# Conditioning vectors 2 to 8 in jobs of 512 columns with raw buffers of their own

## The chip, the cores and the metric

The kernel runs on one core of one Trainium2 chip. A core has TensorE (PE, matrix products into PSUM), VectorE (DVE), ScalarE (ACT), GpSimd (POOL) and SyncE (SP), which here issues nearly all DMAs from one queue, in order. PEld is PE's weight load, which overlaps its matmuls. The metric is the device time of one execution in microseconds (us), lower is better.

## The reference

One layer of a diffusion backbone over 512 latent tokens and 256 context tokens, all float32, with model width 1024 and feed-forward width 2816. Nine conditioning vectors of width 1024 (shift, scale and gate for each of three sub-layers) come from one matrix:

```python
def adaln(cond, w_mod, b_mod):
    m = jax.nn.silu(cond) @ w_mod + b_mod
    return jnp.split(m, N_MOD, axis=-1)

def ffn_sublayer(h, mods, pre_g, post_g, w_gate, w_up, w_down):
    shift, scale, gate = mods
    y = swiglu(modulate(rms_norm(h, pre_g), shift, scale), w_gate, w_up, w_down)
    return h + 0.5 * gate * rms_norm(y, post_g)
```

The layer is a first feed-forward on latent and context tokens (vectors 0 to 2), a mixer of attention and convolution (3 to 5), and a second feed-forward on latent tokens alone (6 to 8). The latent tokens are conditioned by `c`, the context tokens by `c_ctx`. Vectors 0 and 1 are needed at once. Vectors 2, 3 and 4 are needed for both conditions, 5 to 8 for the latent one only.

## The kernel before

**Precision.** Each float32 product is made of three matmuls on float32r halves: `hi` (line 62, ScalarE) rounds a tensor, `lo` (line 67, VectorE) takes the rest, and `wx` (line 92) multiplies hi by hi, hi by lo and lo by hi. Every weight tile therefore goes through a DMA into a raw buffer (tag `wraw`, 4 buffers of 128x1024), a ScalarE copy (`whi`, 4 buffers), a VectorE subtraction (`wlo`, 4 buffers), and then PE. `unit` (line 74) does this; its DMA is line 77.

**Order.** The tile framework builds each engine's list of instructions itself. It goes by the order in which the code is written and by its own estimates of when operands and buffers are free, so an instruction can run ahead of its place. On the chip each engine and SyncE's queue then work through their list in order.

**The first feed-forward.** The 22 chunks of 128 hidden columns form groups of 6, 6, 6 and 4. `gate_up1(f)` (line 405) makes chunk f: weights `f1gu`, sums `pa`, `pb` (latent, 512 columns) and `pc` (context, 256 columns), then silu, product, and the halves `hh` and `hl`. After a group, the first chunk of the next group is made, and then the down-projection adds the group's part of the eight output blocks: the loop over `d` at line 517, with weights `f1d` and sums in PSUM tags `pd` and `pc`, two buffers each, emptied by VectorE into `yl` and `yc` (lines 523 to 527). In the last group, chunks 20 and 21 are made for the context columns first (shorter matmuls), then the context blocks are projected (line 531), chunks 20 and 21 are made for the latent columns (line 540), and the latent blocks follow (line 554). Meanwhile the context's norm, residual and modulation run as `chain` (`sandwich`, line 1026).

**The conditioning of vectors 2 to 8.** It isn't a matmul: for one column block, VectorE multiplies each of the eight raw row blocks of the matrix by a column of `sc` (silu of the condition, one number per partition) and adds them up; PE then sums over the partitions by multiplying with ones; and VectorE picks each column's sum by a product with the identity and a reduction. The work is cut into 20 jobs of two accumulators of 256 columns (line 435). For vectors 2 to 4 the two are the latent and the context condition of the same columns (two raw loads of 512 KB). For 5 to 8 they are two column blocks of the latent condition (four raw loads). `mod_unit` (line 439) loads into the `wraw` buffers (line 448), does 16 operations of 256 columns (lines 455 and 458), and splits the result (`mah`, `mal`). `mod_spread` (line 473) does the two matmuls with ones into a `pd` buffer, two masked products (line 480) and two sums (line 484), and, at a vector's last block, adds the bias and makes the scale or gate. `mod_step` (line 467) spreads the job before and begins the next one. It is called after each of the chunks 2 to 21, twice after chunk 4 (line 512).

Of the kernel before, what the change touches and what calls it, by code (L numbers as in the profile page):

```python
# [16 lines left out]
P = 128  # L17
DM = 1024
ND = 8
# [20 lines left out]
class Builder:  # L40
# [142 lines left out]
    def build(self):  # L183
# [248 lines left out]
            self.lo(hl[:, c0:c1], a[:, c0:c1], hh[:, c0:c1])  # L432
            return h

        mod_jobs = [[(m, d, 0), (m, d, 1)] for m in (2, 3, 4) for d in range(0, ND, 2)]
        mod_jobs += [[(m, d, 0), (m, d + 2, 0)] for m in (5, 6, 7, 8) for d in (0, 4)]
        pend = []

        def mod_unit():

            job = mod_jobs.pop(0)
            acc = self.t(fp, [P, 2, 256], "macc")
            raws = {}
            for hf in range(2):
                for i, (m, d, v) in enumerate(job):
                    if (m, d, hf) not in raws:
                        raw = raws[m, d, hf] = self.t(self.wp, [P, DM], "wraw", bufs=self.n_raw)
                        nc.sync.dma_start(out=raw, in_=io["wmod"][8 + (m - 2) * 4 + d // 2, hf])
                    raw = raws[m, d, hf]
                    for k in range(4):  # L450
                        kk = hf * 4 + k
                        s = sc[:, 2 * kk + v:2 * kk + v + 1]
                        src = raw[:, k * 256:k * 256 + 256]
                        if kk == 0:
                            nc.vector.tensor_scalar(out=acc[:, i], in0=src, scalar1=s,
                                                    scalar2=None, op0=ALU.mult)
                        else:
                            nc.vector.scalar_tensor_tensor(out=acc[:, i], in0=src, scalar=s,  # L458
                                                           in1=acc[:, i], op0=ALU.mult,
                                                           op1=ALU.add)  # L460
            ah = self.t(fp, [P, 2, 256], "mah", F32R)
            al = self.t(fp, [P, 2, 256], "mal", F32R)
            self.hi(ah, acc)
            self.lo(al, acc, ah)
            pend.append((job, ah, al))

        def mod_step():
            if pend:
                mod_spread(*pend.pop(0))
            if mod_jobs:  # L470
                mod_unit()

        def mod_spread(job, ah, al):
            pm = self.t(psf, [P, 2, 256], "pd", bufs=2)
            self.mm(pm, self.ones_r, ah, True, False)
            self.mm(pm, self.ones_r, al, False, True)
            for i, (m, d, v) in enumerate(job):
                mods = (ml, mcx)[v]
                j = self.t(fp, [P, 2, P], "mdj")
                nc.vector.tensor_tensor(  # L480
                    out=j, in0=pm[:, i].rearrange("p (i n) -> p i n", i=2),
                    in1=self.ident.unsqueeze(1).to_broadcast([P, 2, P]), op=ALU.mult)
                c0 = m * 8 + d
                nc.vector.tensor_reduce(out=mods[:, c0:c0 + 2], in_=j, axis=AX.X, op=ALU.add)
                if d != 6:
                    continue
                nc.vector.tensor_tensor(
                    out=mods[:, m * 8:m * 8 + 8], in0=mods[:, m * 8:m * 8 + 8],
                    in1=vec[:, V_BM + m * 8:V_BM + m * 8 + 8], op=ALU.add)
                if m == 2:  # L490
                    make_gate((gp1, gp1c)[v], mods, 2, V_POST1, 0.5)
                elif m == 4:
                    make_scale((sml, smc)[v], mods, 4, V_MPRE)
                elif m == 5:
                    make_gate(gpm, ml, 5, V_MPOST, 1.0)
                elif m == 7:
                    make_scale(s2l, ml, 7, V_PRE2)
                elif m == 8:
                    make_gate(gp2, ml, 8, V_POST2, 0.5)
# [8 lines left out]
        for gi, g in enumerate(groups):  # L508
            for f in g:
                if f not in hs:  # L510
                    hs[f] = gate_up1(f, (f not in late, True))
                for _ in range(0 if f < 2 else 2 if f == 4 else 1):
                    mod_step()
            if gi + 1 < len(groups):
                f = groups[gi + 1][0]
                hs[f] = gate_up1(f)
                for d in range(ND):
# [7 lines left out]
                    else:  # L525
                        nc.vector.tensor_tensor(out=yl[d], in0=yl[d], in1=pl, op=ALU.add)
                        nc.vector.tensor_tensor(out=yc[d], in0=yc[d], in1=pc[:, :NCX], op=ALU.add)
        while mod_jobs or pend:
            mod_step()
        sqyc = self.sqsum(fp, NCX)  # L530
        for d in range(ND):
            w = self.unit(wsl(d), len(g) * P)
# [25 lines left out]
        for half in range(2):  # L558
            c = slice(half * 256, half * 256 + 256)
            for d in range(NFULL, ND):  # L560
                if half == 0:
                    tags = (("hh", HB), ("hl", HB)) if d + 1 < ND else (("macc", 1), ("mah", 1))
                    wd[d] = self.unit(wsl(d), len(g) * P, [
                        self.t(fp, [P, NT], tag, F32R, bufs=bufs) for tag, bufs in tags])
                down1(d, wd[d], c)
# [533 lines left out]
def _layout(inp):  # L1099
# [15 lines left out]
    arr["vec"] = np.ascontiguousarray(np.concatenate(vec, axis=1))  # L1115
    wm = f("w_mod")[0]
    first = wm[:, :2048].reshape(DM, 2, ND, P).transpose(0, 2, 1, 3).reshape(DM, 2048)
    arr["wmod"] = np.concatenate([_wide(first, 8), _wide(wm[:, 2048:], 28)], axis=0)
    for l, n in (("f1", "ffn1"), ("f2", "ffn2")):
        g = _blocks(f(f"{n}_w_gate")[0], NF)  # L1120
        u = _blocks(f(f"{n}_w_up")[0], NF)
# [44 lines left out]
```

## Time and profile before

| | |
|---|---|
| time, 3 runs | 1680.52 us median, 1679.67 to 1681.71 |
| the profiled execution | 1680.81 us, of which the span is 1679.0 |
| mean granted clock of PE | 0.992 |
| conditioning loads from `wmod` into `wraw` | 56 of 512 KB, 3.7 us each from issue to landing |
| conditioning multiply-adds, line 458 | from 64.3 to 553.5 us |
| first feed-forward, chunks and down-projections | about 60 to 620 us |

The lines of the profile that the argument needs stand in the prediction. Three forms occur. A line of a timeline gives start, duration, engine, line, operation, output and inputs, shape and, in brackets, the idle time before it with what ended that. A line of waits gives who waited for whom, total us, how often, and the longest. A line of a group gives the count, the busy us together, the mean ns of one, and the idle time before.

### The profile page before, as it was taken

The page shows a single profiled execution, that of the slowest core. Times are in us where ns is not written, and L with a number is a line of the kernel's source. Part 1 is how long each engine was busy: PE and PEld are TensorE (multiplying, and loading weights), DVE is VectorE, ACT ScalarE, POOL GpSimd, SP SyncE. Part 2 cuts the span into 40 slices and gives each one's busy share as a digit, 9 for nine tenths or more (in the row PEclk, how much of TensorE's full clock was granted, in tenths as well). Part 3 has the DMA queues.
Part 4 walks back from the last instruction along what each step waited for, and adds up shares of the span by engine and source line. Part 5 has one row for each costly group of instructions (what it writes and reads, how often), then busy time and mean ns, then how long its engine had stood idle before and what let it go on. Part 6 is the DMA issues. An engine that isn't in the chain of part 4 may idle for free. (4 is left out here: it accounts for less than half of the span.)

```text
span 1679.0 us, 23556 instructions
## 1 busy us (share of the span) xinstructions
PE 1616.9 (96%) x9154; PEld 1405.3 (84%) x9154; DVE 998.1 (59%) x1699; ACT 647.7 (39%) x1050; POOL 132.3 (8%) x126
## 2 busy tenths in 40 slices
PE   5999999999999988999999999999999999999996
PEld 4887888888888878889888888788889998888886
DVE  5656467456745789577777776473347843343345
ACT  5322122112211556355555555442237732222234
POOL 2100000000000135100000000000002100000003
PEclk9999999999999999999999999999999999999999
DMA  9233333235433547854545442732246743232321
GB/s 374 81 112 101 106 120 105 83 97 193 157 120 103 169 137 243 251 167 124 146 121 163 120 132 95 252 128 96 92 151 195 258 132 120 82 107 91 97 76 51
DMA packets 95248, 232.85 MB, mean 139 GB/s; under 512 B 10912, under 2 KB 34592, under 8 KB 95136
## 3 DMA queue, kind: packets, MB, share of 16 engines
q1 hardware_dynamic: 95136, 231.34, 43.3%
q8 instruction: 72, 1.18, 0.3%
q14 instruction: 40, 0.33, 0.1%
HBM read 201.94 MB, written 16.78 MB: 130 GB/s over the span
## 5 line engine op out<-in xcount | busy, mean ns | idle before, releaser
L62 ACT CAST whi<-wraw 128x1024 fp32r<-128x1024 f32 (+2 forms) x274 | 271.8, 993 | 594.1 <-PE pc L90 174.9
L67 DVE TENSOR_TENSOR wlo<-wraw,whi 128x1024 fp32r<-128x1024 f32 (+2 forms) x264 | 325.8, 1236 | 181.9 <-ACT whi L62 178.1
L90 PE MATMUL pa<-xhi,wlo 128*128 128x512 f32 (+1 forms) x520 | 193.8, 373 | 4.8 <-DVE wlo L67 4.8
L90 PE MATMUL pa<-xhi,whi 128*128 128x512 f32 (+1 forms) x520 | 193.9, 373 | 0.5 <-ACT ob L777 0.5
L90 PE MATMUL pa<-xlo,whi 128*128 128x512 f32 (+1 forms) x520 | 193.3, 372 | 0.0
L90 PE MATMUL pb<-xhi,wlo 128*128 128x512 f32 (+1 forms) x392 | 143.7, 367 | 0.3 <-DVE wlo L67 0.3
L90 PE MATMUL pb<-xhi,whi 128*128 128x512 f32 (+1 forms) x392 | 143.8, 367 | 0.0
L90 PE MATMUL pb<-xlo,whi 128*128 128x512 f32 (+1 forms) x392 | 143.0, 365 | 0.0
L90 PE MATMUL f<-xhi,whi 128*128 128x512 f32 x320 | 127.2, 397 | 0.0
L90 PE MATMUL f<-xhi,wlo 128*128 128x512 f32 x320 | 124.9, 390 | 0.0
L90 PE MATMUL pd<-hh,whi 128*128 128x512 f32 x304 | 121.2, 399 | 3.5 <-ACT hh L62 3.2
L90 PE MATMUL f<-xlo,whi 128*128 128x512 f32 x320 | 124.6, 389 | 0.0
L458 DVE SCALAR_TENSOR_TENSOR macc<-wraw,sc,macc 128x256 f32<-128x256 f32 x280 | 118.4, 481 | 5.3 <-DMA wraw<-wmod 4.3
L90 PE MATMUL pd<-hh,wlo 128*128 128x512 f32 x304 | 120.2, 395 | 0.0
L90 PE MATMUL pd<-hl,whi 128*128 128x512 f32 x304 | 119.2, 392 | 0.0
L90 PE MATMUL pc<-xchi,whi 128*128 128x256 f32 x384 | 109.4, 285 | 4.9 <-ACT whi L62 3.6
L90 PEld LDWEIGHTS pa<-xhi,whi 128*128 128x128 f32 x520 | 98.1, 189 | 17.6 <-ACT ob L777 0.7
L90 PEld LDWEIGHTS pa<-xhi,wlo 128*128 128x128 f32 x520 | 98.4, 189 | 16.7 <-DVE wlo L67 5.5
L90 PE MATMUL pc<-xchi,wlo 128*128 128x256 f32 x384 | 109.3, 285 | 3.0 <-DVE wlo L67 3.0
L90 PE MATMUL pc<-xclo,whi 128*128 128x256 f32 x384 | 109.0, 284 | 0.0
L90 PEld LDWEIGHTS pa<-xlo,whi 128*128 128x128 f32 x520 | 98.2, 189 | 11.6
L90 PEld LDWEIGHTS pc<-xchi,whi 128*128 128x128 f32 x384 | 73.4, 191 | 19.0 <-ACT whi L62 4.0
(313 smaller groups left out, 3287.1 us busy)
## 6 DMA issues: line engine op xcount, KB each, us to landing
wraw<-wmod SPq DMA_DIRECT2D x56, 512.0 KB, 3.7
wraw<-f2gu SPq DMA_DIRECT2D x56, 512.0 KB, 3.5
wraw<-f1gu SPq DMA_DIRECT2D x48, 512.0 KB, 3.8
wraw<-f1d SPq DMA_DIRECT2D x24, 384.0 KB, 3.2
wraw<-f2d SPq DMA_DIRECT2D x24, 384.0 KB, 3.1
wm<-wmod SPq DMA_DIRECT2D x16, 512.0 KB, 9.7
wraw<-wk SPq DMA_DIRECT2D x16, 512.0 KB, 3.9
wraw<-wv SPq DMA_DIRECT2D x16, 512.0 KB, 3.9
```

Source lines behind the costliest of these rows:

```text
L62: self.nc.scalar.copy(out=out, in_=src)
L67: (eng or self.nc.vector).tensor_tensor(out=out, in0=src, in1=hi.bitcast(F32), op=ALU.subtract)
L90: self.nc.tensor.matmul(out, lhsT=lhsT, rhs=rhs, start=start, stop=stop)
L458: nc.vector.scalar_tensor_tensor(out=acc[:, i], in0=src, scalar=s, in1=acc[:, i], op0=ALU.mult, op1=ALU.add)
```

## The change

The jobs get 512 columns. For vectors 2 to 4, a job is half of the row blocks of 512 columns under both conditions (two raw loads, eight operations), so that two jobs make one column block; for 5 to 8, a job is all row blocks of 512 columns under the latent condition (four raw loads, eight operations). There are 12 + 8 = 20 jobs, as before. The raw loads go into a tag of their own, `mraw`, with two buffers, and the accumulators into `vch`, also two. The halves use `tmp` and `sqacc512_0` and `sqacc512_1`, which later work uses too. The spread handles 512 columns with one masked product and one sum of 512; `mod_step` now spreads all that is pending, which is two accumulators after the second job of a pair. Steps are called after chunks 2 to 17, once each, and within the first three down-projections after blocks d=2 and d=5: 22 calls. In the host's layout the matrix for vectors 2 to 8 is a tensor of its own, `wmodr`, in pieces of two row blocks of 512 columns.

```diff
-        mod_jobs = [[(m, d, 0), (m, d, 1)] for m in (2, 3, 4) for d in range(0, ND, 2)]
-        mod_jobs += [[(m, d, 0), (m, d + 2, 0)] for m in (5, 6, 7, 8) for d in (0, 4)]
-        pend = []
+        mod_jobs = [(m, q, (0, 1), r) for m in (2, 3, 4) for q in range(2) for r in ((0, 1), (2, 3))]
+        mod_jobs += [(m, q, (0,), (0, 1, 2, 3)) for m in (5, 6, 7, 8) for q in range(2)]
+        accs, pend = {}, []
...
+            m, q, vs, rs = mod_jobs.pop(0)
+            for v in vs:
+                if rs[0] == 0:
+                    accs[v] = self.t(fp, [P, 512], "vch", bufs=2)
+            for r in rs:
+                raw = self.t(fp, [P, 2, 512], "mraw", bufs=2)
+                nc.sync.dma_start(out=raw, in_=io["wmodr"][(m - 2) * 2 + q, r])
+                for k in range(2):
+                    kk = 2 * r + k
+                    for v in vs:
                         s = sc[:, 2 * kk + v:2 * kk + v + 1]
...
+            if rs[-1] == 3:
+                for v in vs:
+                    ah = self.t(fp, [P, 512], "tmp", F32R, bufs=3)
+                    al = self.t(fp, [P, NT], f"sqacc{NT}_{v}", F32R)
+                    self.hi(ah, accs[v])
+                    self.lo(al, accs[v], ah)
+                    pend.append((m, q, v, ah, al))
 
         def mod_step():
-            if pend:
+            while pend:
                 mod_spread(*pend.pop(0))
...
-        def mod_spread(job, ah, al):
-            pm = self.t(psf, [P, 2, 256], "pd", bufs=2)
+        def mod_spread(m, q, v, ah, al):
+            pm = self.t(psf, [P, 512], "pd", bufs=2)
             self.mm(pm, self.ones_r, ah, True, False)
             self.mm(pm, self.ones_r, al, False, True)
...
+            j = self.t(fp, [P, 512], "tmp", bufs=3).rearrange("p (i n) -> p i n", i=4)
+            nc.vector.tensor_tensor(
+                out=j, in0=pm.rearrange("p (i n) -> p i n", i=4),
+                in1=self.ident.unsqueeze(1).to_broadcast([P, 4, P]), op=ALU.mult)
+            c0 = m * 8 + 4 * q
+            nc.vector.tensor_reduce(out=mods[:, c0:c0 + 4], in_=j, axis=AX.X, op=ALU.add)
+            if q == 1:
...
-                for _ in range(0 if f < 2 else 2 if f == 4 else 1):
+                if 1 < f < NF - 4:
                     mod_step()
...
                         nc.vector.tensor_tensor(out=yl[d], in0=yl[d], in1=pl, op=ALU.add)
                         nc.vector.tensor_tensor(out=yc[d], in0=yc[d], in1=pc[:, :NCX], op=ALU.add)
-        while mod_jobs or pend:
-            mod_step()
+                    if d in (2, 5):
+                        mod_step()
+        assert not mod_jobs and not pend
...
-                    tags = (("hh", HB), ("hl", HB)) if d + 1 < ND else (("macc", 1), ("mah", 1))
+                    tags = (("hh", HB), ("hl", HB)) if d + 1 < ND else (("mraw", 2), ("mraw", 2))
...
-    arr["wmod"] = np.concatenate([_wide(first, 8), _wide(wm[:, 2048:], 28)], axis=0)
+    arr["wmod"] = _wide(first, 8)
+    a = wm[:, 2048:].reshape(4, 2, P, 14, 512).transpose(3, 0, 2, 1, 4)
+    arr["wmodr"] = np.ascontiguousarray(a)
```

More of the change, by code (lines that the diff above doesn't have):

```diff
@@ L433, in gate_up1 @@
             return h
-        mod_jobs = [[(m, d, 0), (m, d, 1)] for m in (2, 3, 4) for d in range(0, ND, 2)]
-        mod_jobs += [[(m, d, 0), (m, d + 2, 0)] for m in (5, 6, 7, 8) for d in (0, 4)]
-        pend = []
+        mod_jobs = [(m, q, (0, 1), r) for m in (2, 3, 4) for q in range(2) for r in ((0, 1), (2, 3))]
+        mod_jobs += [(m, q, (0,), (0, 1, 2, 3)) for m in (5, 6, 7, 8) for q in range(2)]
+        accs, pend = {}, []
         def mod_unit():
[L441 to L451, printed above, removed]
+            m, q, vs, rs = mod_jobs.pop(0)
[8 more added lines that the diff above has]
+                    for v in vs:
@@ L452, in mod_unit @@
                         s = sc[:, 2 * kk + v:2 * kk + v + 1]
-                        src = raw[:, k * 256:k * 256 + 256]
+                        acc = accs[v]
                         if kk == 0:
-                            nc.vector.tensor_scalar(out=acc[:, i], in0=src, scalar1=s,
+                            nc.vector.tensor_scalar(out=acc, in0=raw[:, k], scalar1=s,
                                                     scalar2=None, op0=ALU.mult)
                         else:
-                            nc.vector.scalar_tensor_tensor(out=acc[:, i], in0=src, scalar=s,
-                                                           in1=acc[:, i], op0=ALU.mult,
-                                                           op1=ALU.add)
@@ L461, in mod_unit @@
[L461 to L465, printed above, removed]
+                            nc.vector.scalar_tensor_tensor(out=acc, in0=raw[:, k], scalar=s,
+                                                           in1=acc, op0=ALU.mult, op1=ALU.add)
+            if rs[-1] == 3:
[5 more added lines that the diff above has]
+                    pend.append((m, q, v, ah, al))
@@ L471, in mod_step @@
                 mod_unit()
-        def mod_spread(job, ah, al):
-            pm = self.t(psf, [P, 2, 256], "pd", bufs=2)
+        def mod_spread(m, q, v, ah, al):
+            pm = self.t(psf, [P, 512], "pd", bufs=2)
             self.mm(pm, self.ones_r, ah, True, False)
             self.mm(pm, self.ones_r, al, False, True)
[L477 to L486, printed above, removed]
+            mods = (ml, mcx)[v]
+            j = self.t(fp, [P, 512], "tmp", bufs=3).rearrange("p (i n) -> p i n", i=4)
[5 more added lines that the diff above has]
+            if q == 1:
                 nc.vector.tensor_tensor(
```

## The prediction

> **What bounds the kernel now.** I read the page first, then TensorE's (PE's) busy time by stage, its waits inside the first feed-forward, and the timeline around each wait.
>
> ```profile
> span 1679.0 us, 23556 instructions
> PE 1616.9 (96%) x9154; PEld 1405.3 (84%) x9154; DVE 998.1 (59%) x1699; ACT 647.7 (39%) x1050; POOL 132.3 (8%) x126
> ```
> ```profile
> 0.00:60.00 60.00, 40.67 (x310) 32.11 (x311) 29.99 (x66) 27.69 (x43) 15.90 (x22) 1.00 0.73 282
> 60.00:540.00 480.00, 476.88 (x2707) 415.43 (x2706) 279.67 (x568) 107.74 (x154) 2.16 (x2) 1.00 0.37 118
> 540.00:740.00 200.00, 180.76 (x1146) 163.04 (x1145) 157.56 (x286) 100.61 (x185) 55.97 (x44) 0.97 0.63 192
> ```
>
> The second fence is the view by stretches: after each stretch and its length stand the busy us of PE, PEld, DVE, ACT and POOL, then the granted clock, the DMA share and GB/s. From 60 to 540 us, where nearly all the conditioning work lies, PE idles 480 - 476.88 = 3.1 us. VectorE (DVE) idles 200 us there. So PE bounds this stage, and VectorE time saved is worth nothing unless PE waits for it. From 540 to 740 PE idles 19.2 us, part of it while the last jobs run. The waits from 40 to 580 us are few:
>
> ```profile
> PE pc L90 <- ACT whi L62: 3.6, 1, 3.6
> PE pa L90 <- DVE wlo L67: 2.9, 1, 2.9
> PE pc L90 <- DVE wlo L67: 0.9, 1, 0.9
> ```
>
> The 2.9 us wait is at 143 us, before chunk 6. PE, then ScalarE, then VectorE:
>
> ```profile
> 142.64 0.50 PE L90 MATMUL pd<-hh,whi 128*128 128x512 f32 x1 [0.22 <-ACT whi L62]
> ...
> 143.33 0.28 PE L90 MATMUL pc<-hl,whi 128*128 128x256 f32 x1
> 146.50 0.50 PE L90 MATMUL pa<-xhi,wlo 128*128 128x512 f32 x1 [2.90 <-DVE wlo L67]
> 146.84 0.28 PE L90 MATMUL pc<-xchi,wlo 128*128 128x256 f32 x1
> 147.55 0.28 PE L90 MATMUL pc<-xclo,whi 128*128 128x256 f32 x1
> 147.67 0.40 PE L90 MATMUL pa<-xhi,wlo 128*128 128x512 f32 x1
> ```
> ```profile
> 134.83 1.05 ACT L62 CAST whi<-wraw 128x1024 fp32r<-128x1024 f32 x1
> ```
> ```profile
> 137.70 2.86 DVE L458 SCALAR_TENSOR_TENSOR macc<-wraw,sc,macc 128x256 f32<-128x256 f32 x7
> 145.23 1.22 DVE L67 TENSOR_TENSOR wlo<-wraw,whi 128x1024 fp32r<-128x1024 f32 x1
> ```
>
> The gate weights of chunk 6 had their high part by 135.9 us, but VectorE made the low part only at 145.23, behind the multiply-adds of a third job: chunk 4 has two steps, so three jobs fall on two chunks. PE starts 256-column matmuls 0.12 us apart (147.55 to 147.67), so after 143.33 it was due at 143.45 and went on at 146.50: 3.05 us. The first matmul took 0.34 us to the next one instead of about 0.23, and at 142.64 there is a wait of 0.22 us. In all **3.4 us**.
>
> The 3.6 us wait is at 545 us, before chunk 20, which has only the 256 context columns:
>
> ```profile
> 528.92 6.08 SPq L448 DMA_DIRECT2D wraw<-wmod  x4
> 544.16 2.57 SPq L77 DMA_DIRECT2D wraw<-f1gu  x2
> ```
> ```profile
> 544.77 0.40 PE L90 MATMUL pd<-mal,ones_r 128*128 128x512 f32 x1
> 548.77 0.58 PE L90 MATMUL pc<-xchi,whi 128*128 128x256 f32 x1 [3.60 <-ACT whi L62]
> 550.47 0.58 PE L90 MATMUL pc<-xchi,wlo 128*128 128x256 f32 x1 [0.90 <-DVE wlo L67]
> 554.48 0.31 PE L90 MATMUL pc<-xchi,wlo 128*128 128x256 f32 x1
> ```
> ```profile
> 550.00:555.00 5.00, 4.53 (x23) 4.53 (x24) 4.33 (x8) 2.90 (x4) 0.00 (x0) 0.55 0.56 156
> ```
>
> Four conditioning loads took all four raw slots, so the weights could only be asked for at 544.16, once the multiply-adds had freed a slot. PE was due at 545.00 and started at 548.77 (3.77 us). It then needed 1.70 us for three short matmuls, worth about 0.36 (1.34 more), and from 550.47 to 554.48 it started 18 matmuls 0.22 us apart instead of 0.12 (18 x 0.12 = 2.16, so 1.85 more): after this wait the granted clock was 0.55. Together **7.0 us**.
>
> The queue's own waits say the same for the whole stage: weight loads (L77) wait mostly for conditioning arithmetic.
>
> ```profile
> SPq L77 <- DVE macc L458: 167.4, 35, 20.7
> SPq L448 <- DVE wlo L67: 108.0, 31, 6.3
> ```
>
> **The change part by part.** The profiled execution took 1680.81 us (span 1679.0 and 1.8 around it), 0.3 above the median of 1680.52. The sum is made against 1680.8.
>
> *Arithmetic on VectorE.*
>
> ```profile
> L458 DVE SCALAR_TENSOR_TENSOR macc<-wraw,sc,macc 128x256 f32<-128x256 f32 x280 | 118.4, 481 | 5.3 <-DMA wraw<-wmod 4.3
> L455 DVE TENSOR_SCALAR macc<-wraw,sc 128x256 f32<-128x256 f32 x40 | 13.7, 361 | 13.5 <-DMA wraw<-wmod 13.5
> L171 DVE SCALAR_TENSOR_TENSOR tmp<-x,s,pbs 128x512 f32<-128x512 f32 x4 | 2.8, 750 | 0.0
> L480 DVE TENSOR_TENSOR mdj<-pd,ident 128x256 f32<-128x256 f32 x40 | 16.7, 419 | 1.9 <-PE pd L90 1.9
> ```
>
> Gone are 320 operations of 256 columns, 118.4 + 13.7 = 132.1 us. In their place come 140 multiply-adds and 20 first products of 512. Four such multiply-adds kept VectorE busy 2.8 us (0.70 each), so 140 x 0.70 = 98; the 20 products lie between 0.34 and 0.72 us each, say 0.55, so 11. That saves about 23 us. The 40 masked products become 20, at the 0.69 us of other 512-column operations: 3 us less, and as much for the 40 sums. Some 29 us of VectorE time go, worth **0** directly: the stage's 200 us of idle VectorE time hide it. Without that cover it would be worth 29.
>
> *Matmuls and DMA bytes.* 20 spreads of two 512-column matmuls before (40), 20 after: **0**. The loads stay 56 of 512 KB: **0** as traffic, at a DMA share of 0.37.
>
> *Raw buffers of their own.* The four weight slots no longer wait for conditioning arithmetic. At 545 us there is in addition no job left: the 22 new steps are four for chunks 2 to 5, two in the down-projection, six for chunks 6 to 11, two, six for 12 to 17, two; the twenty jobs end with chunk 17. The 7.0 us wait goes: next late there is weight loading, 512 KB per 24 x 0.12 = 2.9 us of gate or up matmuls, which wraw's four free slots prefetch during the 17 us of chunk 19 (48 rounds of 0.35). Gain between 5 (some of the 0.9 us for the low part and of its slow clock stays) and 7.0; I take **7.0**.
>
> *Steps moved.* Chunk 4 loses its second step, so one job of 16 multiply-adds (16 x 118.4/280 = 6.8 us) fewer stands ahead of the low part at 145.23; it would come at about 138, before 143.45. Gain between 0 and 3.4; I take **3.4**, since 6.8 exceeds 3.05 twice over.
>
> *What the moved steps add.* Steps behind blocks d=2 and d=5 of the down-projections spread into the PSUM tag pd, which has two buffers and also carries those blocks' sums. Nothing of this is in the trace; the nearest rows are one block's end:
>
> ```profile
> 508.00 0.40 PE L90 MATMUL pd<-hh,wlo 128*128 128x512 f32 x1
> 508.23 0.28 PE L90 MATMUL pc<-hh,wlo 128*128 128x256 f32 x1
> 508.35 0.40 PE L90 MATMUL pd<-hh,whi 128*128 128x512 f32 x1
> ```
> ```profile
> 508.43 0.69 DVE L526 TENSOR_TENSOR yl<-yl,pd 128x512 f32<-128x512 f32 x1 [4.16 <-PE pd L90]
> 509.04 0.41 DVE L527 TENSOR_TENSOR yc<-yc,pc 128x256 f32<-128x256 f32 x1
> ```
>
> Today the next block takes the other buffer and has the whole length of a block as slack (18 rounds of 0.23 + 0.12 us, 6.3 us). With one spread between, that block needs the buffer that is emptied until 509.12; PE would be there at 508.35 + 2 x 0.24 = 508.83 and waits 0.3 us. With two spreads the second waits those 0.3, and the block waits for the first one's masked product, behind both additions: 509.4 + 0.7 = 510.1 against 509.6, 0.5 more. By the order of jobs, two spreads fall into the first and the second down-projection each (after chunks 5 and 11, whose jobs end a pair), one more into the second and one into the third: 2 x 0.8 + 2 x 0.3 = 2.2. If VectorE is in the middle of something, up to 0.7 more each; I take **3**, between 0 (the scheduler finds other matmuls to put between) and 4 x 2.9 = 12 (every event as long as the stall at 143).
>
> Sum: 1680.8 - 7.0 - 3.4 + 3 = 1673.4, or **1673** as a median.
>
> [...]
>
> ```profile
> 620.00:660.00 40.00, 35.15 (x281) 33.74 (x281) 37.59 (x79) 21.21 (x50) 20.41 (x19) 1.00 0.71 219
> ```
>
> PE idled 4.85 us of these 40 in many short waits, at a clock of 1.00.
>
> **The rivals.**
>
> *A, the forecast:* both waits go, the PSUM handover costs some 3: 1670 to 1677. 55%.
>
> *B, it does little:* the separate buffers don't separate the loads, since all still go through the one SyncE queue in order, so a conditioning load that waits for one of only two slots holds the weight loads behind it; or the handover costs near its 12. Then only the 7.0 or less remains: 1680.8 - 7.0 + 3 to 12 = 1677 to 1684 (taken to 1684). For it: the 167.4 us of queue waits above exist already. Against: they hardly ever reached PE. 20%.
>
> *C, more than forecast:* the handover costs nothing (1670.4), and the waits behind 580 us shrink too, with VectorE free earlier:
>
> ```profile
> PE pd L90 <- ACT hh L62: 3.2, 1, 3.2
> ```
>
> At 595 us PE waits for the last chunk's hidden values, with VectorE late by the context chain. If that goes, 1667. Against: the context chain's own work, which holds VectorE there, is untouched. 13%.
>
> *D, slower:* jobs of vectors 5 to 8 put four loads through two buffers. The third load waits in SyncE's queue until VectorE has used the first, and the next weights are asked for behind the fourth. Before, the weights of a chunk lay ready 7 to 8 us ahead of PE in these stretches (low part at 375.97, chunk needed at 383.98). If the queue holds them back by more than that, each of the eight jobs costs one stall as at 143, 8 x 3.4 = 27: 1673 + 27 = 1700; with half of them, 1687. Against: four loads stand ahead of the next weights in the same queue today (528.92, then 544.16), and PE waits for it once in the stage, where a chunk is short. 10%.
>
> ```profile
> 375.97 1.23 DVE L67 TENSOR_TENSOR wlo<-wraw,whi 128x1024 fp32r<-128x1024 f32 x1
> 383.98 0.69 DVE L426 TENSOR_TENSOR silu<-silu,pb 128x512 f32<-128x512 f32 x1 [3.91 <-PE pb L90]
> ```
>
> *E, the clock falls at each handover:* each of the four events then costs the 1.34 + 1.85 = 3.2 us that slow matmuls cost after 545: 1673 + 13 = 1686. 2%, by the row at 620. [...]
>
> **How the numbers follow.** The likeliest is A, 1673.0. The range 1667 to 1683 holds A and C and most of B; D, E and a little of B are left out, 2 in 10 at most. A measurement of this kernel tells about 0.2% (3.4 us) from no change, so faster means below 1677.1, slower above 1683.9. Faster: A 55, C 13, and 6 of B: 74%. Same: 14 of B, 14%. Slower: D and E, 12%.
>
> **What would show it.** Right: in the waits of PE up to 580 us the 3.6 and 2.9 us entries are gone, the clock stays at 1.00 around chunk 20, weight loads no longer wait for macc or its successor, and small waits of pd for VectorE appear inside the three down-projections, each under 1 us. VectorE's busy time falls by some 29 us with nothing to show for it. Wrong: weight loads waiting for the conditioning buffers in SyncE's queue and PE waiting for whi or wlo in chunks 12 to 17 (D); a granted clock under 1.00 there (E); or a gap at chunk 6 that stays, which would mean that VectorE's order and not its load made it. The stages behind 740 us should not move.

## The result and the profile after

The changed kernel takes 1666.53 us (median of 4 runs, 1665.19 to 1668.06), the kernel before, run beside it, 1681.12 (4 runs, 1679.67 to 1683.44): ratio 0.9912, 95% interval 0.9895 to 0.9929. The gain is 14.6 us by the medians; the forecast was 7.5 and 1673. The profiled execution of the changed kernel took 1668.06 us, 12.75 less than that of before (1680.81). It is split up below.

The head of the page after, then the view by stretches (stretch and length; busy us of PE, PEld, DVE, ACT, POOL; granted clock, DMA share, GB/s):

```profile
span 1666.3 us, 23372 instructions
PE 1614.2 (97%) x9154; PEld 1403.5 (84%) x9154; DVE 975.3 (59%) x1499; ACT 646.8 (39%) x1050; POOL 133.7 (8%) x126
```
```profile
60.00:540.00 480.00, 480.00 (x2731) 418.68 (x2730) 270.55 (x404) 109.42 (x158) 2.16 (x2) 1.00 0.38 122
540.00:740.00 200.00, 186.38 (x1185) 167.59 (x1184) 155.33 (x268) 105.67 (x197) 56.60 (x44) 0.98 0.63 191
```

From 60 to 540 us PE is now busy for 480.00 of 480 us at a clock of 1.00: nothing of the conditioning reaches it, neither a late weight nor the moved steps. The whole list of PE's waits from 40 to 580 us is one line, against the three of before with 7.4 us together (and two of 0.2). The wait for the last chunk's hidden values, at 595 us in before, has stayed. The two lines of after:

```profile
PE pc L90 <- DVE silu L426: 0.6, 1, 0.6
```
```profile
PE pd L90 <- ACT hh L62: 3.1, 1, 3.1
```

SyncE's queue shows why. Its timeline has the weights of chunks 19 to 21 (six loads) asked for from 477 us on, the last of them within 32.73 us; in before the last two stood at 544.16. The last conditioning load is issued at 424.6 now. Its waits, from 40 to 580 us, no longer hold a weight load (L77) for conditioning arithmetic: the 167.4 us behind `macc` are gone, and only conditioning loads (L448) wait for `vch`. Weight loads now wait mostly for the low halves of earlier weights, which means that they are ahead.

```profile
477.09 32.73 SPq L77 DMA_DIRECT2D wraw<-f1gu  x6
```
```profile
SPq L77 <- DVE wlo L67: 313.3, 63, 13.5
SPq L448 <- DVE vch L458: 88.6, 54, 5.2
```

**Where the 12.75 us lie.** Three points in PE's timelines divide the span: the first gate matmul, the start behind the wait for `hh`, where the first feed-forward's last projection begins, and the last down-projection matmul of the second feed-forward. Before, then after:

```profile
29.01 0.50 PE L90 MATMUL pa<-xhi,h 128*128 128x512 f32 x1 [1.73 <-ACT xhi L174]
598.63 0.59 PE L90 MATMUL pd<-hh,whi 128*128 128x512 f32 x1 [3.24 <-ACT hh L62]
1666.36 0.28 PE L90 MATMUL pd<-hh,g 128*128 128x256 f32 x1
```
```profile
29.54 0.50 PE L90 MATMUL pa<-xhi,h 128*128 128x512 f32 x1 [1.73 <-ACT xhi L174]
588.98 0.58 PE L90 MATMUL pd<-hh,whi 128*128 128x512 f32 x1 [3.09 <-ACT hh L62]
1653.60 0.28 PE L90 MATMUL pd<-hh,g 128*128 128x256 f32 x1
```

The first stretch went from 569.62 to 559.44 us (-10.2), the second from 1067.73 to 1064.62 (-3.1); the start was 0.5 later. Below, "first stretch" always means the first of these, and "lost" the time between 60 and 580 us by which PE's matmuls start later than their pitch, counted in gaps over 0.2 us.

### The profile page after: what moved, and what is told of

It reads as the page before. It is cut to its first block, busy times and chain, and to the rows that moved or that the text cites. A ratio compares the mean times of both kernels' runs of the same rounds, so it can differ in the third digit from the quotient of the medians.

```text
span 1666.3 us, 23372 instructions
## 1 busy us (share of the span) xinstructions
PE 1614.2 (97%) x9154; PEld 1403.5 (84%) x9154; DVE 975.3 (59%) x1499; ACT 646.8 (39%) x1050; POOL 133.7 (8%) x126
## 5 line engine op out<-in xcount | busy, mean ns | idle before, releaser
L90 PE MATMUL pc<-xchi,wlo 128*128 128x256 f32 x384 | 108.3, 282 | 2.1 <-DVE wlo L67 2.1
L458 DVE SCALAR_TENSOR_TENSOR vch<-mraw,sc,vch 128x512 f32<-128x512 f32 x140 | 99.1, 747 | 17.1 <-DMA mraw<-wmodr 15.6
L165 POOL TENSOR_TENSOR sqacc<-sqacc,sqt 128x256 f32<-128x256 f32 (+1 forms) x23 | 20.7, 901 | 856.4 <-ACT sqt L163 856.4
```

The lines of the kernel that those rows point to most:

```text
L90: self.nc.tensor.matmul(out, lhsT=lhsT, rhs=rhs, start=start, stop=stop)
L165: eng.tensor_tensor(out=a, in0=a, in1=s, op=ALU.add)
L458: nc.vector.scalar_tensor_tensor(out=acc, in0=raw[:, k], scalar=s, in1=acc, op0=ALU.mult, op1=ALU.add)
```

## The experiments

First a correction. The prediction and the expectations call the wait at 545 us that ahead of chunk 20. It stands ahead of chunk 21, the second of the two short ones: in before, ScalarE's silu of a chunk of 256 columns alone comes ahead of it, at 544.73. What is said of its cause isn't touched by that; outside the quoted texts it is called chunk 21 here.

```profile
544.73 0.38 ACT L424 ACTIVATE silu<-pc 128x256 f32<-128x256 f32 x1 [4.45 <-PE pc L90]
```

Three ingredients of the change could each be the cause: raw slots of the conditioning's own, more buffers for its small tiles (accumulator `vch`, halves `tmp` and `sqacc`), and the new places of the steps; a fourth, 512 columns, only makes the arithmetic shorter. Each kernel's ratio is against the kernel before, run beside it. The table sums them up; each stands with its expectation below.

| kernel | median us | ratio, interval | first stretch | lost |
|---|---|---|---|---|
| before (first profile) | 1680.52 | | 569.6 | 9.2 |
| rb_before | 1680.75 | 0.9999 (0.9985 to 1.0013) | 571.8 | 9.2 |
| after | 1666.53 | 0.9912 (0.9895 to 0.9929) | 559.4 | 0.8 |
| ra_after | 1667.66 | 0.9919 (0.9902 to 0.9935) | 559.6 | 0.8 |
| e1_own | 1666.53 | 0.9914 (0.9900 to 0.9928) | 558.7 | 0.3 |
| e2_place | 1665.33 | 0.9916 (0.9901 to 0.9932) | 559.6 | 0.8 |
| e3_shared | 1668.64 | 0.9923 (0.9907 to 0.9939) | 559.5 | 0.8 |
| e4_512 | 1665.52 | 0.9914 (0.9898 to 0.9931) | 558.7 | 0.4 |
| e7_only512 | 1666.26 | 0.9915 (0.9899 to 0.9931) | 558.9 | 0.6 |
| e9_acc | 1667.07 | 0.9917 (0.9901 to 0.9933) | 558.9 | 0.3 |
| g2_vch | 1667.42 | 0.9935 (0.9913 to 0.9956) | 558.8 | 0.3 |
| g5_raw | 1670.06 | 0.9920 (0.9898 to 0.9942) | 560.0 | 1.8 |
| g6_halves | 1666.95 | 0.9916 (0.9891 to 0.9942) | 558.5 | 0.3 |
| e6_take | 1667.71 | 0.9919 (0.9907 to 0.9932) | 558.2 | 0.8 |
| e5_both | 1672.28 | 0.9949 (0.9936 to 0.9962) | 562.7 | 1.3 |
| e10_single | 1674.68 | 0.9957 (0.9943 to 0.9971) | 564.6 | 4.8 |
| e8_order | 1680.21 | 0.9999 (0.9987 to 1.0011) | 573.0 | 11.8 |
| g3_tmp | 1679.92 | 1.0000 (0.9983 to 1.0016) | 572.3 | 9.8 |

The first stretch falls into two groups, 558 to 560 us without the waits and 570 to 573 with them, with two kernels between. The medians follow it.

### Taking the ingredients one by one

**e1_own**: before, with own raw slots and roomier small tiles; 256 columns and the old places.

```diff
-            acc = self.t(fp, [P, 2, 256], "macc")
+            acc = self.t(fp, [P, 2, 256], "vch", bufs=2)
-                        raw = raws[m, d, hf] = self.t(self.wp, [P, DM], "wraw", bufs=self.n_raw)
+                        raw = raws[m, d, hf] = self.t(fp, [P, DM], "mraw", bufs=2)
-            ah = self.t(fp, [P, 2, 256], "mah", F32R)
-            al = self.t(fp, [P, 2, 256], "mal", F32R)
+            ah = self.t(fp, [P, 2, 256], "tmp", F32R, bufs=3)
+            al = self.t(fp, [P, 2, 256], f"sqacc{NT}_0", F32R)
```

> The kernel before with one part of the change: the raw loads of the conditioning jobs go into two buffers of their own (mraw), and the small tiles move into vch, tmp and sqacc512_0 to make room. Jobs of 256 columns and the places of the steps stay as before. Theory OWN (the shared raw slots alone made both waits): the waits of 3.6 us at 545 and of 2.9 us at 143 are gone, 8 to 11 us faster than before, about 1671. Theory PLACE (the steps' places made them): the wait ahead of chunk 20 stays within 1 us of its 7.0, because four-load jobs still stand ahead of its weights in SyncE's queue; at most 3.4 faster. Theory LOAD (VectorE's work made them): no gain, as the 320 operations of 256 columns stay.

**e2_place**: before, with the new places alone.

```diff
-                for _ in range(0 if f < 2 else 2 if f == 4 else 1):
+                if 1 < f < NF - 4:
                     mod_step()
...
-        while mod_jobs or pend:
-            mod_step()
+                    if d in (2, 5):
+                        mod_step()
```

> The kernel before with one other part of the change: the steps stand after chunks 2 to 17 and behind blocks 2 and 5 of the first three down-projections. Shared raw slots and 256-column jobs stay. Theory PLACE: both waits gone, and no new one, 10 us faster, about 1671. Theory OWN: the wait ahead of chunk 20 goes, since no job is left there, but weight loads still wait for multiply-adds, and inside the down-projections, where a block lasts 6.3 us, PE waits for whi or wlo at one or more of the six new places, 3 us each; gain under 5 us.

**e3_shared**: after, with the raws back in the shared slots.

```diff
-                raw = self.t(fp, [P, 2, 512], "mraw", bufs=2)
+                raw = self.t(self.wp, [P, DM], "wraw", bufs=self.n_raw).rearrange("p (k n) -> p k n", k=2)
```

> The changed kernel with the raw loads put back into the four shared weight slots; 512-column operations and the new places stay. Theory PLACE: as the changed kernel within 2 us, about 1667. Theory OWN: 5 to 12 us slower than the changed kernel, with waits of PE for whi or wlo in the down-projections or behind four-load jobs.

**e4_512**: after, with the old places (the two hunks of e2_place undone).

> The changed kernel with the steps at the places of before: once after each of the chunks 2 to 21, twice after chunk 4, and the rest before the last context projection. Own buffers and 512-column operations stay. Theory OWN or LOAD: within 2 us of the changed kernel. Theory PLACE: the wait ahead of chunk 20 comes back in part (four loads through two buffers stand ahead of its weights, which are asked for only after the multiply-adds of the third load), 4 to 8 us slower than the changed kernel.

All four gave the whole gain: 1666.53, 1665.33, 1668.64 and 1665.52 us. e1 and e2 share no ingredient, so neither the slots nor the places can be *the* cause. In e2 weight loads still wait for the accumulator, 124.1 us in all against 167.4 in before, and none of it reaches PE:

```profile
SPq L77 <- DVE macc L458: 124.1, 31, 11.0
```

Theory PLACE of e4, a loss of 4 to 8 us by the old places, fell: 1665.52, with 0.4 us lost.

**rb_before** and **ra_after** are the two kernels once more, unchanged.

> The kernel before, unchanged, profiled once more. Theory SCATTER (what the changed kernel gained behind 680 us differs from execution to execution, since every engine's list of instructions there is the same in both kernels): the wait of PE for VectorE's v, 3.4 us at 687 in the first profile, comes out between 0.3 and 3.6, and the stretch from the first value matmul to the first scores, 39.6 us then, between 35 and 40. Theory SHIFT (the earlier arrival itself makes that stretch shorter): both come out within 0.5 us of the first profile. The waits of 3.6 and 2.9 us in the first feed-forward must come again within 0.3 us.

> The changed kernel, unchanged, profiled once more. Theory SCATTER: its stretch from the first value matmul to the first scores (37.9 us) moves by more than 0.5 us. Theory SHIFT: it stays within 0.5. In the first feed-forward: no wait over 1 us before 580 us, as in its first profile.

The waits are the kernel's own: 3.5, 3.0 and 1.3 us in before again, 0.6 in after. Their cost is less firm: behind the wait before chunk 6 the granted clock stayed at 1.00 in before and fell to 0.74 in rb_before (the lines stand in the last section), and the first stretch is 2.1 us longer there. What lies behind the first feed-forward is not firm either. The second stretch was 1065.35 us in rb_before and 1064.64 in ra_after: 0.7 apart, where the first pair had 3.1. Theory SCATTER holds: PE's wait for `v` came out at 1.4 us in rb_before (3.4 in before), and the stretch from the first value matmul to the first scores at 36.1 (39.6); in ra_after that stretch moved from 37.9 to 36.4.

**e7_only512**: 512 columns with room in the small tiles, but shared slots and the old places (e3_shared and e4_512 together).

> The third part alone: operations of 512 columns and jobs cut as in the change, but the raw loads in the shared weight slots and the steps at the places of before. Theory ANY (each of the three parts alone removes both waits, since each removes one of the conditions under which they arise): within 2 us of the changed kernel, about 1667. Theory QUEUE (own slots or no late job is needed): the wait ahead of chunk 20 stays between 4 and 7 us, since four loads still take all four slots there; the one at chunk 6 goes, as a step has 8 operations of 5.7 us in place of 16 of 6.8; gain 3 to 6 us.

1666.26 us. Both of the other named ingredients can be missing at once. What this kernel still has in common with e1 is the room in the small tiles.

**e9_acc**: before with that alone. The edit is that of e1_own without its `raw` line.

> The kernel before with only the small tiles of the jobs given more room: accumulators in vch (two buffers for one), their halves in tmp (three for one) and sqacc512_0. Raw loads stay in the shared weight slots, jobs stay at 256 columns and at the places of before. e1_own had this as well as the raw buffers of its own. Theory ROOM (a job's arithmetic could not begin before PE had spread the job before, so raw slots stayed taken): both waits gone, about 1667. Theory OWN (it was the raw slots in e1_own): both waits stay, 1680.

1667.07 us, and no wait over 0.2 us in the list of waits. **e10_single** goes the other way: e7_only512 with one accumulator and one high half for each condition.

```diff
-                    accs[v] = self.t(fp, [P, 512], "vch", bufs=2)
+                    accs[v] = self.t(fp, [P, 512], f"macc_{v}")
...
-                    ah = self.t(fp, [P, 512], "tmp", F32R, bufs=3)
+                    ah = self.t(fp, [P, 512], f"mah_{v}", F32R)
```

> e7_only512 (512-column operations, shared raw slots, old places) with one accumulator and one high half for each condition, as before the change, in place of two and three. Theory ROOM: the wait ahead of chunk 20 comes back, 4 to 7 us, about 1673 to 1676. Theory WIDTH (jobs of 8 operations free the slots sooner): no wait over 1 us before 580 us, within 2 us of e7_only512.

1674.68: the wait ahead of chunk 21 is back, that at chunk 6 isn't. PE's waits and SyncE's timeline of e10:

```profile
PE pc L90 <- ACT whi L62: 2.8, 1, 2.8
PE pc L90 <- DVE wlo L67: 0.9, 1, 0.9
```
```profile
525.59 4.88 SPq L448 DMA_DIRECT2D wraw<-wmodr  x4
540.64 1.90 SPq L77 DMA_DIRECT2D wraw<-f1gu  x2
```

**e8_order**: before, with the jobs of vectors 5 to 8 (four loads each) first and the two-load jobs last. It tests whether the wait is made by loads that stand ahead in the queue, as the prediction said.

```diff
-        mod_jobs = [[(m, d, 0), (m, d, 1)] for m in (2, 3, 4) for d in range(0, ND, 2)]
-        mod_jobs += [[(m, d, 0), (m, d + 2, 0)] for m in (5, 6, 7, 8) for d in (0, 4)]
+        mod_jobs = [[(m, d, 0), (m, d + 2, 0)] for m in (5, 6, 7, 8) for d in (0, 4)]
+        mod_jobs += [[(m, d, 0), (m, d, 1)] for m in (2, 3, 4) for d in range(0, ND, 2)]
```

> The kernel before with only the order of its jobs turned round: the eight jobs of four loads (vectors 5 to 8) first, the twelve of two loads (vectors 2 to 4) last. Slots, sizes and places as before. Theory QUEUE: the wait ahead of chunk 20 goes or falls under 2 us, since only two of the four shared slots hold conditioning loads there; gain about 7 us there, and the wait at chunk 6 stays or grows, because the double step after chunk 4 now holds eight loads. Against it (a cause other than the slots): the wait ahead of chunk 20 stays as it is.

The time did not change (1680.21), but the wait moved. Ahead of chunks 21 and 6 it is gone; ahead of chunk 5, whose weights now stand behind the eight raw loads of the two steps after chunk 4, a single one of 7.9 us has come. It takes back the 7 us that were expected. PE's waits and SyncE's timeline:

```profile
PE pa L90 <- ACT whi L62: 7.9, 1, 7.9
```
```profile
89.52 27.33 SPq L448 DMA_DIRECT2D wraw<-wmod  x8
129.47 3.16 SPq L77 DMA_DIRECT2D wraw<-f1gu  x2
```

### What holds a job up

The timelines of before around 500 to 525 us, in the order SyncE, ScalarE, PE, VectorE:

```profile
497.91 13.04 SPq L448 DMA_DIRECT2D wraw<-wmod  x4
525.75 2.31 SPq L77 DMA_DIRECT2D wraw<-f1gu  x2
```
```profile
521.43 0.62 ACT L62 CAST mah<-macc 128x512 fp32r<-128x512 f32 x1 [12.18 <-PE pd L90]
```
```profile
520.99 0.40 PE L90 MATMUL pd<-mah,ones_r 128*128 128x512 f32 x1
```
```profile
522.35 0.68 DVE L67 TENSOR_TENSOR mal<-macc,mah 128x512 fp32r<-128x512 f32 x1
523.27 0.34 DVE L455 TENSOR_SCALAR macc<-wraw,sc 128x256 f32<-128x256 f32 x1
```

The four raw loads issued up to 511 us lie in all four slots. Their first product, which needs `macc`, runs at 523.27. The accumulator is not free because its job isn't split; that isn't split because `mah` and `mal` still hold the job before; and those wait for their spread, which PE reaches at 520.99, behind the down-projection. ScalarE stood 12.18 us for it while the raws landed. Everything behind is late by that: chunk 20's weights at 525.75, the next four raws at 528.92, chunk 21's weights at 544.16. Three more kernels tell which link counts.

**g2_vch**: before with a second accumulator alone (the first line of e1_own's edit). **g3_tmp**: before with three buffers for the high half alone (its `ah` line).

> The kernel before, with only the accumulator moved to two buffers (tag vch); the halves stay single (mah, mal), raws in the shared slots. Theory ACCUMULATOR: it is the next job's first product, which needs an accumulator, that holds the slots; both waits go, 1666 to 1669, ratio 0.992 to 0.993. Theory HALVES: ScalarE and VectorE cannot write the halves of the next job before the spread of this one has read them, and they stand still there with the casts of the weights queued behind; then the waits stay for the most part, 1674 to 1680, ratio 0.996 to 0.999, and ScalarE still waits some 12 us for PE at mah.

> The kernel before, with only the high half moved to three buffers (tag tmp); accumulator single (macc), low half single (mal), raws in the shared slots. Theory HALVES: both waits go for the most part, 1666 to 1670, ratio 0.992 to 0.994, and ScalarE's wait of 12 us at the high half is gone. Theory ACCUMULATOR: the waits stay, 1674 to 1680, ratio 0.996 to 0.999.

g2 gains everything (1667.42), g3 nothing (1679.92). But g3 was no fair test of the halves: the low half still had one buffer. ScalarE, PE and VectorE of g3:

```profile
501.63 0.62 ACT L62 CAST tmp<-macc 128x512 fp32r<-128x512 f32 x1 [2.26 <-DVE macc L458]
```
```profile
524.17 0.40 PE L90 MATMUL pd<-mal,ones_r 128*128 128x512 f32 x1
```
```profile
525.28 0.68 DVE L67 TENSOR_TENSOR mal<-macc,tmp 128x512 fp32r<-128x512 f32 x1
```

The high half came at 501.63, 20 us earlier than in before, and the low half none the earlier. **g6_halves** therefore gives room to both and leaves the accumulator single:

```diff
-            ah = self.t(fp, [P, 2, 256], "mah", F32R)
-            al = self.t(fp, [P, 2, 256], "mal", F32R)
+            ah = self.t(fp, [P, 2, 256], "tmp", F32R, bufs=3)
+            al = self.t(fp, [P, 2, 256], "vch", F32R, bufs=2)
```

> The kernel before, with both halves given room: the high half in tmp (3 buffers), the low half in vch (2 buffers); the accumulator stays single (macc), raws in the shared slots, the old places. In the trace of g3_tmp the high half of the job at 500 us was made at 501.63, but the low half, which has one buffer, only at 525.28, behind the spread of the job before (PE, 524.17), and only then the accumulator was free for the next job. Theory HANDS (the accumulator is held because its low half cannot be written before the spread of the job before has read the old one): with room for both halves the accumulator comes free at once and a single one is enough, both waits go, 1666 to 1671, ratio 0.992 to 0.995. Theory ACCUMULATOR (two accumulators are needed for the next job to start while this one is split): the waits stay, 1676 to 1681, ratio 0.997 to 1.000.

1666.95 us. A single accumulator is enough when both halves can be written before the spread of the job before. In before, g2 and g6 SyncE's list of instructions is the same, entry for entry; only its timing differs. The lists of PE, ScalarE and VectorE are not the same: with the room, the framework also puts their instructions into another order. So g2 and g6 show the room together with the order that follows from it; what the buffer alone would do with the old order is not tested. g6, SyncE:

```profile
508.66 12.70 SPq L448 DMA_DIRECT2D wraw<-wmod  x4
523.79 1.52 SPq L77 DMA_DIRECT2D wraw<-f1gu  x2
```

The last four raw loads and chunk 21's weights are the entries that stood at 528.92 and 544.16 in before, 20 us earlier.

**g5_raw**: own raw slots, with the accumulator and the low half single. Two more 4 KB buffers don't fit beside the old small tiles (g1_raw, with nothing else changed, needs 114.1 KB a partition where 108.7 are left, and so has no time). The small tiles therefore use tags that are idle then; the high half gets three buffers by it, which g3 shows to be worth nothing alone.

```diff
-            acc = self.t(fp, [P, 2, 256], "macc")
+            acc = self.t(fp, [P, 2, 256], f"sqacc{NT}_1")
-                        raw = raws[m, d, hf] = self.t(self.wp, [P, DM], "wraw", bufs=self.n_raw)
+                        raw = raws[m, d, hf] = self.t(fp, [P, DM], "mraw", bufs=2)
-            ah = self.t(fp, [P, 2, 256], "mah", F32R)
-            al = self.t(fp, [P, 2, 256], "mal", F32R)
+            ah = self.t(fp, [P, 2, 256], "tmp", F32R, bufs=3)
+            al = self.t(fp, [P, 2, 256], f"sqacc{NT}_0", F32R)
```

> The kernel before, with the raw loads of the conditioning in two buffers of their own; the accumulator stays single (in sqacc512_1, idle until the jobs are over), the halves go to tmp and sqacc512_0, which g3_tmp gives no gain for (high half). 256 columns, the old places. Theory SLOTS: with slots of their own, weights no longer wait for conditioning arithmetic and both waits go, 1666 to 1670, ratio 0.992 to 0.994. Theory ACCUMULATOR (as g2_vch shows for the other side): the single accumulator still holds the third and fourth load of a job in the queue, with the weights behind them, so the wait ahead of chunk 20 stays or moves, 1674 to 1684, ratio 0.996 to 1.002.

1670.06 us and ratio 0.992, with 1.8 us still lost: own slots (and the high half's room that comes with them) are enough too. The queue still stands for conditioning arithmetic, now at the raw loads themselves, but weights that are ahead of PE by a chunk can bear it. SyncE's waits of g5:

```profile
SPq L448 <- DVE sqacc L458: 184.9, 39, 13.6
```

### The handover in the down-projections

The forecast paid 3 us for spreads between the blocks. The changed kernel's PE at the end of block d=2 of the first down-projection, and VectorE beside it:

```profile
176.16 0.28 PE L90 MATMUL pc<-hh,wlo 128*128 128x256 f32 x1
176.28 0.40 PE L90 MATMUL pd<-tmp,ones_r 128*128 128x512 f32 x1
176.52 0.40 PE L90 MATMUL pd<-sqacc,ones_r 128*128 128x512 f32 x1
176.76 0.28 PE L90 MATMUL pc<-hh,whi 128*128 128x256 f32 x1
176.87 0.28 PE L90 MATMUL pc<-hl,whi 128*128 128x256 f32 x1
176.99 0.28 PE L90 MATMUL pc<-hh,wlo 128*128 128x256 f32 x1
177.11 0.49 PE L90 MATMUL pd<-tmp,ones_r 128*128 128x512 f32 x1
...
177.90 0.40 PE L90 MATMUL pd<-hh,whi 128*128 128x512 f32 x1
```
```profile
176.36 0.69 DVE L522 COPY yl<-pd 128x512 f32<-128x512 f32 x1 [4.68 <-PE pd L90]
176.97 0.68 DVE L480 TENSOR_TENSOR tmp<-pd,ident 128x512 f32<-128x512 f32 x1
```

The second spread needs the buffer that the copy empties until 177.05, and PE starts it at 177.11. Between the two spreads PE does three matmuls of the *next* block's context sum, which needs no `pd` buffer. Two more of them stand ahead of 177.90. The handover costs one step of 0.33 (177.11 to 177.44) instead of 0.23 us. In the whole stage there are four such steps (177.11, 332.55, 352.52 and 488.56), 0.4 us together.

**e5_both** is to take that filler away: each spread in the down-projections is done a second time into a `pc` buffer, with a copy out of it. The result isn't used.

```diff
+            if both[0]:
+                px = self.t(psf, [P, 512], "pc", bufs=2)
+                self.mm(px, self.ones_r, ah, True, False)
+                self.mm(px, self.ones_r, al, False, True)
+                jx = self.t(fp, [P, 512], "tmp", bufs=3)
+                nc.vector.tensor_copy(out=jx, in_=px)
```

> The changed kernel, in which each spread inside the down-projections is followed by a second, unused one into the tag pc (two matmuls and a copy by VectorE), so that the next block can begin neither its latent nor its context sums at once. Six spreads, 6 x 0.48 = 2.9 us of matmuls added. Theory FILL (the handover of the pd buffers cost nothing because PE takes the next block's context matmuls in between): waits of PE for VectorE appear at those places, 0.3 to 1.0 us each, 2 to 4 us in all on top of the 2.9. Theory NONE (the buffers are emptied in time anyway): no wait there over 0.2 us; only the 2.9 us more.

The first stretch grew by 3.2 us against after, hardly more than the added matmuls alone (12 of 0.23 to 0.24 us, 2.8), and only one new wait of over 0.2 us is in the profile:

```profile
PE pc L90 <- DVE tmp L485: 0.3, 1, 0.3
```

So the waits that theory FILL expected did not come, and the result is that of NONE but for this one. But the added spread gives VectorE time as well, 0.47 us each, so that it is a filler itself; whether the bare handover would have cost the 0.3 to 0.8 of the forecast stays open.

**e6_take** asks whether the 3.1 us wait for the last chunk's hidden values can go. It is after, with the context chain's steps all taken behind chunk 20:

```diff
-            take(chain, 6)
+            take(chain, 6 if f == late[0] else 0)
```

> A try for a faster version: the changed kernel, in which the context chain takes six steps behind the first of the two late chunks and none behind the second (before: six behind each), so that VectorE is freer for the last chunk's hidden values. Expected: the wait of 3.1 us of PE for hh at 586 us shrinks under 2 and the slow matmuls behind it go, 2 to 5 us faster than the changed kernel, unless the chain, which the context keys need, becomes late by as much.

The wait fell to 1.8 and the time did not move (1667.71), so the expected 2 to 5 us did not come: PE then waits 0.8 us for `hl` and 0.7 us for the context's norm.

## Why the prediction was wrong, and where it was right

**The failed step is the handover term**, "I take 3, between 0 (the scheduler finds other matmuls to put between) and 12". Measured: no wait at all and 0.4 us in four slower steps; PE is busy for 480.00 of 480 us. The small waits of `pd` that were named as a sign did not come. I had counted when the buffer would come free against the next block's *first latent* matmul, though that block has 18 context matmuls that need no `pd` buffer, and the timeline shows PE taking some of them there, the lower bound's own reason. That the 3 us would have been paid without them is not shown (e5_both). Without the term the sum is 1670.4.

**The two waits** (7.0 and 3.4 us, together 10.4) both went, and their sizes fit the profile from which they were read: the first stretch got shorter by 10.2 us in the first pair. In the repeats it was 12.2, mostly because the same wait before chunk 6 was followed by a lowered clock in rb_before (0.74), some 1.5 us more, and not in before (1.00): 3.4 was the lower of the two prices that these executions show for this wait. (A slip in the 7.0: the 1.70 us behind 548.77 hold two short matmuls, not three, 0.1 us more.) That weights stand behind raw loads in one queue is shown by e8_order (eight raw loads from 89.52 us on, chunk 5's weights at 129.47, a wait of 7.9 us). What the prediction gave as its remedy, raw slots of their own, is one of four that do it: slots (g5_raw), a second accumulator (g2_vch), room for both halves (g6_halves), or new places (e2_place). I did not follow the 12.2 us for which ScalarE stood at `mah`, which the waits of before have. They point to the root, a job whose halves can't both be written before the spread of the job before; they aren't the root themselves, since g3_tmp does away with them and gains nothing. The 3.4 us at chunk 6 were put down to the double step after chunk 4. e9_acc keeps that step and loses the wait, with chunk 6's gate low part made at 121.5 us in another order of VectorE's list (145.2 in before), so the step isn't enough for it. Whether it was needed isn't shown: e2_place, where it is gone, moves the other steps as well.

**"The stages behind 740 us should not move"** did not hold in the first pair of profiles, where the second stretch (from 598.63 and 588.98 us on) gave 3.1 us. That isn't the change's doing as far as the runs show. From the first feed-forward's last projection on, every engine's list of instructions is the same in both kernels but for a buffer's name. In before, rb_before, g3_tmp and e8_order, which have such waits, the second stretch took 1060.9 to 1067.7 us; in the twelve profiles that have neither wait and no added matmuls, 1061.7 to 1068.4.

**What is left of the 14.6 us.** The forecast gave the first stretch 10.4 - 3 = 7.4 us. The mean of the twelve profiles just named is 559.1 us, that of before, rb_before and g3_tmp 571.2: 12.2 us. Of the 4.8 us between, 3 are the handover term and the rest is mostly the clock behind the wait before chunk 6, which was 1.00 from 145 to 150 us in before, 0.74 in rb_before and lowered in g3_tmp too (0.56). The ratios of these twelve rows of the table come to 13.7 us on average; where the other 1.5 us lie, less than the interval of a single ratio, stays open.

**VectorE's time** fell as forecast and was worth nothing by itself: e9_acc, e2_place and g2_vch keep all 320 operations of 256 columns and gain as much. The groups after:

```profile
L458 DVE SCALAR_TENSOR_TENSOR vch<-mraw,sc,vch 128x512 f32<-128x512 f32 x140 | 99.1, 747 | 17.1 <-DMA mraw<-wmodr 15.6
L480 DVE TENSOR_TENSOR tmp<-pd,ident 128x512 f32<-128x512 f32 x20 | 13.5, 681 | 0.0
L455 DVE TENSOR_SCALAR vch<-mraw,sc 128x512 f32<-128x512 f32 x20 | 9.2, 479 | 1.8 <-DMA mraw<-wmodr 1.8
```

132.1 us became 99.1 + 9.2 = 108.3 (forecast 98 + 11), the masked products went from 16.7 to 13.5 and the sums from 16.6 to 13.6: 30.0 us together, where 29 were forecast. The page's total fell by 22.8 us only (998.1 to 975.3): it counts once the time in which operations of different groups overlap, while adding the groups counts it in each (all of VectorE's groups add up to 1065.9 us in before and 1034.7 in after).

**The rivals.** D (a jam in SyncE's queue by four loads through two buffers) has its condition in the trace, L448 waiting 88.6 us for `vch`, and never reached PE, since weights were ahead. E did not come: the granted clock is 1.00 from 60 to 540 us. C said what happened to the handover, and its 1667 is close to the measured time. That is luck in part: its second half, the wait at 595 us, stayed.

## What to carry to other kernels

When a load waits in an in-order queue, follow the wait past the buffer to the last link: here it led from a weight slot over an accumulator and its single-buffered halves to a matmul that PE reached 12 us later, and room at one link, 2 KB a partition for a second accumulator, removed both waits (together with the order that the framework made of it). Before paying for a PSUM handover, look for matmuls of the next block that need another buffer (here PE did such matmuls at the four handovers, which together cost 0.4 us; what they cost without stays open). And repeat the profile of before: here the untouched second stretch came out between 1060.9 and 1067.7 us in the four profiles with such waits, more scatter than the 3 us in dispute, and the first stretch, with the same wait before chunk 6, was 2.1 us longer in one execution of before than in the other.

## What the runs showed of the hardware

Behind one and the same wait the granted clock fell in one execution and not in another. The wait before chunk 6 ends at 146.50 us in before (2.90 us; its line stands in the prediction) and at 145.97 in rb_before. The view by stretches of before, then PE's timeline and the view of rb_before:

```profile
145.00:150.00 5.00, 3.50 (x19) 3.05 (x20) 4.76 (x8) 1.46 (x2) 0.00 (x0) 1.00 0.62 168
```
```profile
145.97 0.50 PE L90 MATMUL pa<-xhi,wlo 128*128 128x512 f32 x1 [3.03 <-DVE wlo L67]
```
```profile
145.00:150.00 5.00, 4.03 (x16) 3.45 (x17) 4.55 (x6) 1.24 (x2) 0.00 (x0) 0.74 0.68 188
```

In the values' projection PE waits 1.8 us in both executions of after. PE's timeline and the view by stretches of after, then of ra_after:

```profile
680.57 0.39 PE L90 MATMUL f<-whi,xhi 128*128 128x256 f32 x1 [1.81 <-DVE v L67]
...
681.78 0.41 PE L90 MATMUL f<-whi,xlo 128*128 128x256 f32 x1
682.00 0.41 PE L90 MATMUL f<-whi,xhi 128*128 128x256 f32 x1
...
684.56 0.41 PE L90 MATMUL f<-whi,xhi 128*128 128x256 f32 x1
```
```profile
680.00:690.00 10.00, 9.43 (x58) 9.06 (x59) 3.35 (x9) 3.07 (x6) 0.00 (x0) 0.83 1.04 288
```
```profile
682.64 0.39 PE L90 MATMUL f<-whi,xhi 128*128 128x256 f32 x1 [1.82 <-DVE v L67]
```
```profile
680.00:690.00 10.00, 8.18 (x62) 7.72 (x62) 4.21 (x10) 5.08 (x9) 0.00 (x0) 1.00 1.02 281
```

In after, matmuls of 256 columns start 0.21 us apart instead of 0.12 from 681.57 to 684.77, one us behind the end of the wait, and the granted clock of the 10 us is 0.83; behind the same wait in ra_after it is 1.00. So a wait of 1.8 us was followed by a lowered clock once and once not, and the wait before chunk 6 by one in rb_before (3.03 us, 0.74) and by none in before (2.90 us, 1.00). The measured price of such a wait holds for the execution that was measured; what sets the clock, these runs do not show.
